# High and low weight halves made by GpSimd's DMAs instead of ScalarE and VectorE, in a decoder block on one core

## The chip, the cores and the metric

The kernel runs on one core of a Trainium2 chip. The metric is device time in microseconds (us) of one execution; a figure for a kernel is the median over its runs. The profile comes from one execution, taken by the hardware profiler. Engines are named as in the profile: PE (TensorE matmul), PEld (its weight load), DVE (VectorE), ACT (ScalarE), POOL (GpSimd), SP (SyncE, which here only issues DMAs).

## The reference

One decoder layer on 512 tokens of width 1024, all in float32. Cut to what matters:

```python
h  = rms_norm(x, norm_mix_g)
glu_in, q, k, v, g, gate_logits = split(h @ w_in)
a  = conv31(glu_in[:, :1024] * sigmoid(glu_in[:, 1024:]))     # causal, depthwise
y_a = silu(layer_norm(a)) @ w_conv_proj + conv_proj_b
r  = retention(rotary(q) / 16, rotary(k), v)                   # 4 heads, dk 256, dv 512
y_b = (silu(g) * head_norm(r) * ret_norm_g) @ w_ret_proj
x  = x + (sigmoid(gA) * y_a + sigmoid(gB) * y_b) @ w_out
u  = conv3(rms_norm(x, norm_ffn_g) @ w_up)                     # causal, depthwise
x  = x + (silu(u[:, :3072]) * u[:, 3072:]) @ w_down
return rms_norm(x, norm_final_g)
```

All matrices together are 24.1 million weights, 96.5 MB in float32.

## The kernel before, in words

**Layout.** Activations lie transposed: 128 features on the partitions, 512 tokens in a row. A product is made in *units*: one PSUM bank of 128 output features by 512 tokens, summed over the K blocks of 128 input features (`unit`, L142).

**Split numbers.** PE multiplies in the type float32r, which keeps fewer digits than float32. So each weight and each activation is kept as two float32r tiles, the value rounded (high half, `whi`, `xg` and others) and the rest (low half, `wlo`), and each product is three matmuls: high by high, high by the activation's low half, low by high (L146 to L148).

**The weight stream.** The host lays the weights out in the order of use, in 184 pieces ("halves" in the code) of 128 x 1024 floats, 512 KB each, eight 128 x 128 blocks. One piece feeds 24 matmuls, for most products just one unit. `load_half` (L92) lets SP load a piece into a tile `wraw` (3 buffers). `split_half` (L99) lets ACT round it into `whi` (L105, 3 buffers) and DVE subtract that from `wraw` into `wlo` (L106, 3 buffers). `blocks` (L118) hands out the blocks and, when piece h comes into use, makes sure that pieces up to h + 2 have been asked for (`LOOK = 2`). A buffer comes free when PE has done the last matmul that reads it. Pieces 0 and 1 are asked for at the start, between the loads of x.

**Order.** A scheduler orders the instructions of each engine by priority and its own idea of when they are ready; each engine then works its list strictly in order, and an instruction that waits holds up all that stand behind it on its engine. The pieces have a raised priority (`WPRIO`), the taps of the 31-tap convolution a much lowered one (L337, 30 DVE instructions for each of 8 channel blocks), so that they fill what DVE has left.

**Stages.** For each of four heads: two gated channel blocks (4 units) and their convolution taps, q and k with rotation, the projection of the head before, values, scores, the gate, the retention products. Then the gates, the projections, `w_out`, 28 units of `w_up`, half of `w_down`, 20 more units of `w_up`, the rest of `w_down`, the last norm. Each norm needs a sum over partitions: PE adds with a matrix of ones (L190), DVE scales, POOL takes the power -0.5 (L206), DVE splits, and a unit later PE spreads the result over the partitions (L221). POOL otherwise only clears the few columns ahead of each convolution's input (`ap`, 3 buffers, L327 and L551); that waits until the taps that read the buffer before are done.

Of the kernel before, what the change touches and what calls it, by code (L numbers as in the profile page):

```python
# [9 lines left out]
F32 = mybir.dt.float32  # L10
F32R = mybir.dt.float32r
AF = mybir.ActivationFunctionType
ALU = mybir.AluOpType

P = 128
# [10 lines left out]
FK = 3  # L26
EPS = 1e-6
HS = 8 * P
LOOK = 2
WARM = 9  # L30
WPRIO = 100

# columns of the packed per-feature parameters
_PC = {}
_n = 0
for _name, _w in (
# [11 lines left out]
def hybrid_block(  # L48
# [10 lines left out]
    nc = tc.nc  # L59
    sb = ctx.enter_context(tc.tile_pool(name="sb", bufs=1))  # L60
# [3 lines left out]
    def nm(s):  # L64
        uid[0] += 1
        return f"{s}_{uid[0]}"

    def t512(tag, bufs, dt=F32):
        return sb.tile([P, S], dt, tag=tag, bufs=bufs, name=nm(tag))
# [4 lines left out]
    def bank():  # L74
        return psp.tile([P, S], F32, tag="ps", name=nm("ps"))

    def f32(ap):
        return ap.bitcast(F32)
# [4 lines left out]
        c = _PC[name] + i  # L83
        return par[:, c:c + 1]

# [1 line left out]
    halves = {}  # L87
    emitted = [0]

    raws = {}  # L90

    def load_half(h):  # L92
        raw = sb.tile([P, HS], F32, tag="wraw", bufs=3, name=nm("wraw"))
        cut = (0, 2 * P, HS) if h == 0 else (0, HS)
        raws[h] = raw, [slice(u, v) for u, v in zip(cut, cut[1:])]
        for sl in raws[h][1]:
            nc.sync.dma_start(out=raw[:, sl], in_=wst[h][:, sl])

    def split_half(h):  # L99
        raw, sls = raws.pop(h)  # L100
        hi = sb.tile([P, HS], F32R, tag="whi", bufs=3, name=nm("whi"))
        lo = sb.tile([P, HS], F32R, tag="wlo", bufs=3, name=nm("wlo"))
        with tc.high_priority(offset=WPRIO if h > 1 else 0):
            for sl in sls:
                nc.scalar.copy(out=hi[:, sl], in_=raw[:, sl])  # L105
                nc.vector.tensor_tensor(out=lo[:, sl], in0=raw[:, sl], in1=f32(hi[:, sl]),  # L106
                                        op=ALU.subtract)
        halves[h] = (hi, lo)

    def upto(h):  # L110
        while emitted[0] <= min(h, NBLK - 1):
            load_half(emitted[0])
            split_half(emitted[0])
            emitted[0] += 1

    pos = [0]
# [1 line left out]
    def blocks(n):  # L118
        b = pos[0]
        pos[0] += n  # L120
        h, c = divmod(b, 8)
        upto(h + LOOK)
        hi, lo = halves[h]
        sl = slice(c * P, (c + n) * P)
        return hi[:, sl], lo[:, sl]
# [3 lines left out]
    def later(n, fn):  # L129
        pending.append([n, fn])  # L130
# [42 lines left out]
    def split_scaled(src, g, tag, bufs):  # L173
        h = t512(tag, bufs, F32R)
        l = t512(tag, bufs, F32R)
        nc.scalar.activation(out=h, in_=src, func=AF.Copy, scale=g)
        nc.vector.scalar_tensor_tensor(
            out=l, in0=src, scalar=g, in1=f32(h), op0=ALU.mult, op1=ALU.subtract)
        return h, l
# [1 line left out]
    def add_into(acc, v):  # L181
        nc.vector.tensor_tensor(out=acc, in0=acc, in1=v, op=ALU.add)  # L182

# [1 line left out]
    def tok_sums(ps, parts, chunks=range(NCH), at=0):  # L185
        """The sums of parts over their partitions: token c * 128 + p's at [p, at + c]."""
        last = len(parts) - 1
        for c in chunks:
            for i, (ss, o) in enumerate(parts):
                nc.tensor.matmul(ps[:, at + c:at + c + 1], lhsT=ss[:, c * P - o:(c + 1) * P - o],  # L190
                                 rhs=ones[:, 0:1], start=i == 0, stop=i == last)

    def tok(dt=F32):
        if dt == F32R:
            return sb.tile([P, NCH], F32R, tag="tokr", bufs=4, name=nm("tokr"))
        return sb.tile([P, NCH], F32, tag="tok", bufs=8, name=nm("tok"))

    def scaled(ps, n, eps, sl=slice(0, NCH)):
        o = tok()
        nc.vector.tensor_scalar(out=o[:, sl], in0=ps[:, sl], scalar1=1.0 / n, scalar2=eps,  # L200
                                op0=ALU.mult, op1=ALU.add)
        return o

    def rsqrt(v, sl=slice(0, NCH)):
        r = tok()
        nc.gpsimd.tensor_tensor(out=r[:, sl], in0=v[:, sl], in1=neghalf[:, sl], op=ALU.pow)  # L206
        return r

    def spread_ps(ps, r, chunks=range(NCH)):
        """r's value of each token, on every partition."""  # L210
        sl = slice(chunks[0], chunks[-1] + 1)
        rh = tok(F32R)
        rl = tok(F32R)
        nc.vector.tensor_copy(out=rh[:, sl], in_=r[:, sl])
        nc.vector.tensor_tensor(out=rl[:, sl], in0=r[:, sl], in1=f32(rh[:, sl]), op=ALU.subtract)

        def run():
            for c in chunks:
                dst = ps[:, c * P:(c + 1) * P]
                for i, x in enumerate((rh, rl)):  # L220
                    nc.tensor.matmul(dst, lhsT=x[:, c:c + 1].broadcast_to([P, P]), rhs=identr,  # L221
                                     start=i == 0, stop=i == 1)
            return ps

        return run
# [4 lines left out]
        return b  # L230

    def stat(ss, n, eps, use, wait=(2, 1)):
        """use(spread, per token) of rsqrt(sum / n + eps), or of the mean where eps is None."""
        def second():
            ps = bank()
            tok_sums(ps, [(ss, 0)])
            v = scaled(ps, n, eps or 0.0)
            r = v if eps is None else rsqrt(v)
            run = spread_ps(ps, r)
            later(wait[1], lambda: use(run, r))  # L240

        later(wait[0], second)

# [1 line left out]
    ones = sb.tile([P, P], F32, tag="ones", name="ones")  # L245
    nc.gpsimd.memset(ones, 1.0)
    neghalf = sb.tile([P, NCH], F32, tag="neghalf", name="neghalf")
# [8 lines left out]
    for i in range(KT):  # L256
        t = t512("x", 8)
        nc.sync.dma_start(out=t, in_=xT[i * P:(i + 1) * P, :])
        xs.append(t)
        if i == 0:  # L260
            nc.sync.dma_start(out=g0, in_=params[:, _PC["norm_mix_g"]:_PC["norm_mix_g"] + KT])
            load_half(0)
        if i == 3:
            load_half(1)
    ident = sb.tile([P, P], F32, tag="ident", name="ident")
    nc.sync.dma_start(out=ident, in_=ident_in)
    nc.sync.dma_start(out=par, in_=params)
# [2 lines left out]
    xg = []  # L270
    for i in range(KT):
        xg.append(split_scaled(xs[i], g0[:, i:i + 1], "xg", 16))
        if i in (0, 3):
            split_half(emitted[0])
            emitted[0] += 1

# [31 lines left out]
        nc.vector.tensor_tensor(out=t, in0=ps, in1=rB[0], op=ALU.mult)  # L308
        return t

# [1 line left out]
    PAD = CONV_K - 1  # L312
    accs = [None] * KT
    csum = [None]
# [9 lines left out]
    def glu(ta, sg):  # L324
        nc.scalar.activation(out=sg, in_=sg, func=AF.Sigmoid)
        a = sb.tile([P, S + PAD], F32, tag="ap", bufs=3, name=nm("ap"))
        nc.gpsimd.memset(a[:, 0:PAD], 0.0)  # L327
        nc.vector.tensor_tensor(out=a[:, PAD:], in0=ta, in1=sg, op=ALU.mult)
        return a
# [39 lines left out]

        stat(csum[0], D, None, centre, (3, 2))  # L370

# [1 line left out]
    def rope():  # L373
        p1 = unit(bank(), xg)
        p2 = unit(bank(), xg)
        res = []
        for u, v, op in ((p1, p2, ALU.subtract), (p2, p1, ALU.add)):
            m1 = tmp()
            m2 = tmp()
            nc.vector.tensor_tensor(out=m1, in0=u, in1=cosr, op=ALU.mult)  # L380
            nc.vector.tensor_tensor(out=m2, in0=v, in1=sinr, op=ALU.mult)
            nc.vector.tensor_tensor(out=m1, in0=m1, in1=m2, op=op)
            res.append(split(m1, "A", 16))
        return res
# [97 lines left out]
            else:  # L482
                add_into(yb[m], ps)

# [1 line left out]
    stat(ss.acc, D, EPS, norm_mix)  # L486
    rg = None
    for h in range(H):
        ps = [glu_units() for _ in range(2)] if h else glu_first()
        for i in range(2):  # L490
            a = glu(*ps[i])
# [50 lines left out]
        x1g.append(split_scaled(x_, pcol("norm_ffn_g", m), "A", 16))  # L542
        ss.add(x_)

# [1 line left out]
    def norm_ffn(run, _):  # L546
        rB[0] = spread(run, "rB", 1)

# [68 lines left out]
    def finish(half):  # L617
# [7 lines left out]
        def early(sqs):  # L625
            for q in sqs:
                add_into(ss.acc[:, tk], q[:, :HT])
            tok_sums(ps, [(ss.acc, 0)], chunks)
            part.append(scaled(ps, D, EPS, sl))

        def first(sqs):
            tok_sums(ps, [(sqs[-1], half * HT)], chunks, NCH)
            v = tok()
            nc.vector.scalar_tensor_tensor(
                out=v[:, sl], in0=ps[:, NCH + sl.start:NCH + sl.stop], scalar=1.0 / D,
                in1=part[0][:, sl], op0=ALU.mult, op1=ALU.add)
            run.append(spread_ps(ps, rsqrt(v, sl), chunks))
# [22 lines left out]

# [1 line left out]
def _units(w):  # L662
    """Blocks of 128 output features, each with its K rows: (n, 128, K/128 * 128)."""
    k, n = w.shape
    return w.reshape(k // P, P, n // P, P).transpose(2, 1, 0, 3).reshape(n // P, P, k)

# [94 lines left out]
```

## Time and profile before

| | |
|---|---|
| runs | 1097.77 and 1098.85 us, median 1098.31 us |
| span of the profiled execution, first to last instruction | 1096.1 us |
| median of the runs less this span | 2.2 us |
| PE busy | 1084.7 us, 99% of the span |
| DVE busy | 760.4 us, 69% |
| ACT busy | 419.9 us, 38% |
| POOL busy | 20.5 us, 2% |
| DMA queue of SP | 104.69 MB, 29.0% of 16 DMA engines' time |

How to read it: the span is what the trace covers; the 2.2 us beside it are what the timed runs have on top of it. A busy PE is not PE at its peak, since matmuls overlap in the pipeline. Waiting, issuing a DMA and branching do not count as busy.

### The profile page before, as it was taken

To read this page: it belongs to the slowest core of one execution; us is meant where nothing else is said; L and a number is where in the kernel's file an instruction comes from. 1 tells how busy PE (TensorE), PEld (TensorE's weight loads), DVE (VectorE), ACT (ScalarE), POOL (GpSimd) and SP (SyncE) were. 2 spreads that over 40 slices of the span, in tenths; PEclk is the share of its full clock that TensorE was granted. 3 is DMA by queue.
4 is the path that set the end of the run, shared out by engine and by line. 5 is a ranking of instruction groups with operands and counts; after the bars stand their busy time and mean duration, and the time that the engine had idled before them with its cause. 6 is when DMAs were issued, how large, how long until landed. Compare 5 with 4: busy or idle time off the path is not lost.

```text
span 1096.1 us, 12567 instructions
## 1 busy us (share of the span) xinstructions
PE 1084.7 (99%) x4946; PEld 895.9 (82%) x4946; DVE 760.4 (69%) x1070; ACT 419.9 (38%) x555; POOL 20.5 (2%) x72
## 2 busy tenths in 40 slices
PE   8999999999999999999999999999999999999997
PEld 7888888888888888888888888888888888888886
DVE  6999699739995699938664555577676226767433
ACT  6343332534233331535552334444443113444331
POOL 1000000000000000000000000000000000000000
PEclk9999999999999999999999999999999999999998
DMA  7232132222222232222232432222232222233212
GB/s 271 97 97 87 62 111 91 93 68 86 97 96 87 71 102 96 78 77 77 84 109 94 138 122 100 84 97 97 96 97 92 94 92 90 94 97 96 96 58 77
DMA packets 32475, 105.48 MB, mean 96 GB/s; under 512 B 3616, under 2 KB 5920, under 8 KB 32416
## 3 DMA queue, kind: packets, MB, share of 16 engines
q1 hardware_dynamic: 32416, 104.69, 29.0%
q8 instruction: 38, 0.62, 0.2%
q14 instruction: 21, 0.17, 0.1%
HBM read 102.58 MB, written 2.10 MB: 95 GB/s over the span
## 4 chain that ended last, share of the span: by engine, by line
PE 97%; issue 1%; DVE 1%; DMA 0%; SPq 0%; ACT 0%; POOLq 0%; POOL 0%; DVEq 0%
PE ps L146 28%; PE ps L148 27%; PE ps L147 27%; PE ps L393 3%; PE ps L395 3%; PE ps L394 3%; PE ps L451 1%; PE ps L452 1%; PE ps L450 1%; PE ps L221 1%; PE ps L190 1%; PE ps L429 0%; PE ps L427 0%; PE ps L425 0%; DMA wraw<-in_wst_dram 0%
## 5 line engine op out<-in xcount | busy, mean ns | idle before, releaser
L105 ACT CAST whi<-wraw 128x1024 fp32r<-128x1024 f32 (+1 forms) x185 | 193.6, 1047 | 427.8 <-PE ps L147 296.3
L106 DVE TENSOR_TENSOR wlo<-wraw,whi 128x1024 fp32r<-128x1024 f32 (+1 forms) x185 | 225.0, 1216 | 71.0 <-ACT whi L105 70.2
L146 PE MATMUL ps<-xg,whi 128*128 128x512 f32 x672 | 263.4, 392 | 0.0
L148 PE MATMUL ps<-xg,wlo 128*128 128x512 f32 x672 | 261.8, 390 | 0.0
L147 PE MATMUL ps<-xg,whi 128*128 128x512 f32 x672 | 261.5, 389 | 0.0
L146 PE MATMUL ps<-A,whi 128*128 128x512 f32 x448 | 177.1, 395 | 0.0
L148 PE MATMUL ps<-A,wlo 128*128 128x512 f32 x448 | 177.0, 395 | 0.0
L337 DVE SCALAR_TENSOR_TENSOR C<-ap,par,C 128x512 f32<-128x512 f32 x240 | 166.3, 745 | 3.1 <-ACT C L334 2.7
L147 PE MATMUL ps<-A,whi 128*128 128x512 f32 x384 | 151.7, 395 | 0.0
L148 PEld LDWEIGHTS ps<-xg,wlo 128*128 128x128 f32 x672 | 126.1, 188 | 27.0
L147 PEld LDWEIGHTS ps<-xg,whi 128*128 128x128 f32 x672 | 126.2, 188 | 25.9
L146 PEld LDWEIGHTS ps<-xg,whi 128*128 128x128 f32 x672 | 126.2, 188 | 25.7
L148 PEld LDWEIGHTS ps<-A,wlo 128*128 128x128 f32 x448 | 84.0, 187 | 20.5
L146 PEld LDWEIGHTS ps<-A,whi 128*128 128x128 f32 x448 | 84.0, 187 | 20.4
L147 PEld LDWEIGHTS ps<-A,whi 128*128 128x128 f32 x384 | 72.0, 187 | 17.6
L308 DVE TENSOR_TENSOR t<-ps,rB 128x512 f32<-128x512 f32 x48 | 32.5, 687 | 72.3 <-PE ps L148 72.3
L558 DVE SCALAR_TENSOR_TENSOR t<-ap,par,t 128x512 f32<-128x512 f32 x96 | 71.5, 749 | 1.6
L182 DVE TENSOR_TENSOR x<-x,ps 128x512 f32<-128x512 f32 (+1 forms) x50 | 33.0, 664 | 54.8 <-PE ps L148 51.0
L552 DVE TENSOR_TENSOR ap<-ps,rB 128x512 f32<-128x512 f32 x48 | 33.0, 692 | 47.3 <-PE ps L148 47.3
L146 PE MATMUL ps<-R,whi 128*128 128x512 f32 x160 | 63.3, 396 | 0.0
L148 PE MATMUL ps<-R,wlo 128*128 128x512 f32 x160 | 63.2, 395 | 0.0
L147 PE MATMUL ps<-R,whi 128*128 128x512 f32 x160 | 63.2, 395 | 0.0
(135 smaller groups left out, 1181.8 us busy)
## 6 DMA issues: line engine op xcount, KB each, us to landing
wraw<-in_wst_dram SPq DMA_DIRECT2D x183, 512.0 KB, 3.3
x<-in_xT_dram SPq DMA_DIRECT2D x16, 256.0 KB, 3.4
out_dram<-t SPq DMA_DIRECT2D x8, 256.0 KB, 2.2
dec<-in_decay_dram SPq DMA_DIRECT2D x4, 256.0 KB, 2.6
t<-in_cs_dram SPq DMA_DIRECT2D x2, 256.0 KB, 4.7
wraw<-in_wst_dram SPq DMA_DIRECT2D x1, 384.0 KB, 4.0
par<-in_params_dram SPq DMA_DIRECT2D x1, 264.0 KB, 6.2
wraw<-in_wst_dram SPq DMA_DIRECT2D x1, 128.0 KB, 3.5
```

The source lines that it names most:

```text
L105: nc.scalar.copy(out=hi[:, sl], in_=raw[:, sl])
L106: nc.vector.tensor_tensor(out=lo[:, sl], in0=raw[:, sl], in1=f32(hi[:, sl]), op=ALU.subtract)
L146: nc.tensor.matmul(ps, lhsT=wh, rhs=xh, start=kt == 0, stop=False)
L147: nc.tensor.matmul(ps, lhsT=wh, rhs=xl, start=False, stop=False)
L148: nc.tensor.matmul(ps, lhsT=wl, rhs=xh, start=False, stop=kt == last)
L182: nc.vector.tensor_tensor(out=acc, in0=acc, in1=v, op=ALU.add)
L337: nc.vector.scalar_tensor_tensor(out=acc, in0=a[:, k:k + S], scalar=wcol(k), in1=acc, op0=ALU.mult, op1=ALU.add)
L393: nc.tensor.matmul(banks[c], lhsT=xh[:, sl], rhs=wh, start=kt == 0, stop=False)
L394: nc.tensor.matmul(banks[c], lhsT=xl[:, sl], rhs=wh, start=False, stop=False)
L395: nc.tensor.matmul(banks[c], lhsT=xh[:, sl], rhs=wl, start=False, stop=kt == KT - 1)
L552: nc.vector.tensor_tensor(out=u[:, FK - 1:], in0=ps, in1=rB[0], op=ALU.mult)
L558: nc.vector.scalar_tensor_tensor(out=c, in0=u[:, k:k + S], scalar=wcol(k), in1=c, op0=ALU.mult, op1=ALU.add)
```

## The change

Only piece 0 still comes through `wraw`, ACT and DVE (`ON_ENGINES = 1`; `wraw` keeps one buffer). Pieces 1 to 183 go through `split_by_dma`: a DMA that GpSimd issues reads the piece from memory and writes it as float32r into `whi`; ACT writes the negated `whi` into `wlo`; a second DMA of GpSimd reads the same piece from memory again and adds it onto `wlo`. `whi` and `wlo` have four buffers each instead of three, and `LOOK` is 3. ACT's rounding (1024 columns) has thus become a negation (1024 columns), and DVE's subtraction is gone for 183 pieces; SP issues 183 fewer DMAs and POOL 366 more, and the weights are read from memory twice.

```diff
-LOOK = 2
+LOOK = 3
+ON_ENGINES = 1
...
-        raw = sb.tile([P, HS], F32, tag="wraw", bufs=3, name=nm("wraw"))
+        raw = sb.tile([P, HS], F32, tag="wraw", bufs=ON_ENGINES, name=nm("wraw"))
...
+    def w_tiles():
+        return (sb.tile([P, HS], F32R, tag="whi", bufs=LOOK + 1, name=nm("whi")),
+                sb.tile([P, HS], F32R, tag="wlo", bufs=LOOK + 1, name=nm("wlo")))
+
     def split_half(h):
         raw, sls = raws.pop(h)
-        hi = sb.tile([P, HS], F32R, tag="whi", bufs=3, name=nm("whi"))
-        lo = sb.tile([P, HS], F32R, tag="wlo", bufs=3, name=nm("wlo"))
-        with tc.high_priority(offset=WPRIO if h > 1 else 0):
...
+    def split_by_dma(h):
+
+        hi, lo = w_tiles()
+        with tc.high_priority(offset=WPRIO):
+            nc.gpsimd.dma_start(out=hi, in_=wst[h])
+            nc.scalar.activation(out=lo, in_=f32(hi), func=AF.Copy, scale=-1.0)
+            nc.gpsimd.dma_start(out=lo, in_=wst[h], accum_op=ALU.add)
         halves[h] = (hi, lo)
 
     def upto(h):
         while emitted[0] <= min(h, NBLK - 1):
-            load_half(emitted[0])
-            split_half(emitted[0])
+            split_by_dma(emitted[0])
             emitted[0] += 1
...
-        if i == 3:
-            load_half(1)
...
-        if i in (0, 3):
+        if i == 0:
             split_half(emitted[0])
```

**Where the instructions stand.** POOL's list at the start, before the change: after the first clearings it has only the identity's cast and the first power.

```order
L327 MEMSET ap_1166 128x30
L269 CAST identr<-ident 128x128
L206 ISA
L206 TENSOR_TENSOR tok_243<-tok_241,neghalf 128x4
L327 MEMSET ap_1203 128x30
```

POOL's list at the same place with the change; `whi_170`, `whi_175` and `whi_180` are pieces 1 to 3, `whi_209` is piece 4 and `whi_252` piece 5.

```order
L336 MEMSET ap_1150 128x30
L117 DMA whi_170<-in_wst_dram 128x1024
L117 DMA whi_175<-in_wst_dram 128x1024
L117 DMA whi_180<-in_wst_dram 128x1024
L119 DMA wlo_171<-in_wst_dram 128x1024
L119 DMA wlo_176<-in_wst_dram 128x1024
L119 DMA wlo_181<-in_wst_dram 128x1024
L117 DMA whi_209<-in_wst_dram 128x1024
L278 CAST identr<-ident 128x128
L117 DMA whi_252<-in_wst_dram 128x1024
L119 DMA wlo_210<-in_wst_dram 128x1024
L217 TENSOR_TENSOR tok_245<-tok_243,neghalf 128x4
```

The three casting DMAs of pieces 1 to 3 are issued before anything that waits; the adding ones follow behind ACT's negations; the identity's cast and the first power now stand behind DMAs.

ACT's list at the start with the change, from the rounding of piece 0 (`whi_108`) on; `xg` are the high halves of the scaled x, and `t_144` the first of the squares for the norm.

```order
L108 CAST whi_108<-wraw_82 128x768
L187 ACTIVATE xg_114<-x_85,g_78 128x512
L292 ACTIVATE t_144<-x_85 128x512
L187 ACTIVATE xg_118<-x_87,g_78 128x512
L118 ACTIVATE wlo_171<-whi_170 128x1024
L187 ACTIVATE xg_122<-x_89,g_78 128x512
L118 ACTIVATE wlo_176<-whi_175 128x1024
L187 ACTIVATE xg_126<-x_91,g_78 128x512
L118 ACTIVATE wlo_181<-whi_180 128x1024
L187 ACTIVATE xg_130<-x_93,g_78 128x512
L292 ACTIVATE t_147<-x_87 128x512
```

Before, one instruction of this size (the rounding of piece 1) stood among the eight `xg`, and the squares stood between them; now three negations stand there, and five of the squares come after the last `xg`.

POOL's list among the 28 units of `w_up`, before the change: clearings only.

```order
L551 MEMSET ap_5730 128x2
L551 MEMSET ap_5737 128x2
L551 MEMSET ap_5812 128x2
L551 MEMSET ap_5819 128x2
```

The same place with the change, for one pair of units (pieces `whi_5715` and `whi_5745`) and the start of the next.

```order
L117 DMA whi_5715<-in_wst_dram 128x1024
L560 MEMSET ap_5854 128x2
L117 DMA whi_5745<-in_wst_dram 128x1024
L119 DMA wlo_5716<-in_wst_dram 128x1024
L560 MEMSET ap_5861 128x2
L119 DMA wlo_5746<-in_wst_dram 128x1024
L117 DMA whi_5795<-in_wst_dram 128x1024
```

The first piece's adding DMA stands behind the second piece's casting one, and both stand behind clearings that wait for DVE's taps.

## Rows read from the trace of the kernel before

**Rows 1.** The page: span, busy time by engine, chain that ended last.
```profile
span 1096.1 us, 12567 instructions
PE 1084.7 (99%) x4946; PEld 895.9 (82%) x4946; DVE 760.4 (69%) x1070; ACT 419.9 (38%) x555; POOL 20.5 (2%) x72
...
PE 97%; issue 1%; DVE 1%; DMA 0%; SPq 0%; ACT 0%; POOLq 0%; POOL 0%; DVEq 0%
```

**Rows 2.** PE's waits, longest: line, released by, us in total, times, longest.
```profile
PE ps L221 <- DVE tokr L214: 1.2, 1, 1.2
PE ps L253 <- POOL neghalf L248: 1.0, 1, 1.0
...
PE ps L160 <- DVE xg L177: 0.9, 2, 0.6
```

**Rows 3.** Windows: busy time by engine, granted PE clock, DMA share, GB/s.
```profile
0.00:20.00 20.00, 16.77 (x76) 13.47 (x77) 14.14 (x20) 15.80 (x24) 1.95 (x10) 1.00 0.77 279
...
900.00:1000.00 100.00, 100.00 (x430) 80.41 (x429) 66.36 (x82) 40.08 (x50) 1.62 (x16) 1.00 0.29 95
```

**Rows 4.** Groups by form: busy us, mean ns of one, idle before and its releasers.
```profile
L106 DVE TENSOR_TENSOR wlo<-wraw,whi 128x1024 fp32r<-128x1024 f32 x183 | 223.6, 1222 | 69.8 <-ACT whi L105 69.0 <-issue 0.3
...
L105 ACT CAST whi<-wraw 128x1024 fp32r<-128x1024 f32 x183 | 192.4, 1052 | 426.7 <-PE ps L147 296.3 <-issue 75.1 <-PE ps L394 45.3
```

**Rows 5.** DMA: SP's queue, and two issues (count, KB, us to landing).
```profile
q1 hardware_dynamic: 32416, 104.69, 29.0%
...
wraw<-in_wst_dram SPq DMA_DIRECT2D x183, 512.0 KB, 3.3
...
par<-in_params_dram SPq DMA_DIRECT2D x1, 264.0 KB, 6.2
```

**Rows 6.** Timeline of ACT among the units of `w_up`: start, duration.
```profile
760.93 1.05 ACT L105 CAST whi<-wraw 128x1024 fp32r<-128x1024 f32 x1 [1.17 <-PE ps L147]
...
766.53 1.05 ACT L105 CAST whi<-wraw 128x1024 fp32r<-128x1024 f32 x1 [0.46 <-PE ps L147]
...
772.13 1.05 ACT L105 CAST whi<-wraw 128x1024 fp32r<-128x1024 f32 x1 [1.17 <-PE ps L147]
```

**Rows 7.** Timeline at the start: SP's issue and ACT.
```profile
4.02 0.43 SPq L97 DMA_DIRECT2D wraw<-in_wst_dram  x1
...
6.17 0.83 ACT L105 CAST whi<-wraw 128x768 fp32r<-128x768 f32 x1 [0.60 <-DMA wraw<-in_wst_dram]
...
10.32 1.03 ACT L105 CAST whi<-wraw 128x1024 fp32r<-128x1024 f32 x1
...
15.20 0.71 ACT L176 ACTIVATE xg<-x,g 128x512 fp32r<-128x512 f32 x1
```

**Rows 8.** Timeline at the start: PE, and DVE's subtraction of piece 1.
```profile
8.71 0.50 PE L160 MATMUL ps<-xg,whi 128*128 128x512 f32 x1 [0.30 <-DVE xg L177]
...
11.70 1.22 DVE L106 TENSOR_TENSOR wlo<-wraw,whi 128x1024 fp32r<-128x1024 f32 x1
...
13.64 0.50 PE L160 MATMUL ps<-xg,whi 128*128 128x512 f32 x1 [0.56 <-DVE xg L177]
...
15.15 0.39 PE L160 MATMUL ps<-xg,whi 128*128 128x512 f32 x1
...
18.83 0.95 PE L190 MATMUL ps<-ones,ss 128*128 128x1 f32 x8
```

**Rows 9.** Timeline of POOL.
```profile
106.80 0.12 POOL L327 MEMSET ap<- 128x30 f32 x1 [2.33 <-DVE C L337]
120.56 1.01 POOL L206 TENSOR_TENSOR tok<-tok,neghalf 128x4 f32<-128x4 f32 x1 [13.64 <-DVE tok L200]
...
206.29 0.12 POOL L327 MEMSET ap<- 128x30 f32 x1 [9.15 <-DVE C L337]
243.51 1.96 POOL L206 TENSOR_TENSOR tok<-tok,neghalf 128x4 f32<-128x4 f32 x1 [37.09 <-DVE tok L200]
```

**Rows 10.** Timeline of PE: a norm's sum and spread, and head 1's first gate unit.
```profile
119.34 0.94 PE L190 MATMUL ps<-ones,ss 128*128 128x1 f32 x8
...
125.73 1.01 PE L221 MATMUL ps<-identr,tokr 128*128 128x128 f32 x8
...
201.81 0.46 PE L146 MATMUL ps<-xg,whi 128*128 128x512 f32 x1
```

**Rows 11.** Timeline of ACT at the end: the last piece's rounding.
```profile
1067.20 1.05 ACT L105 CAST whi<-wraw 128x1024 fp32r<-128x1024 f32 x1 [4.43 <-PE ps L147]
```

More of the change, by code (lines that the diff above doesn't have):

```diff
@@ L97, in load_half @@
             nc.sync.dma_start(out=raw[:, sl], in_=wst[h][:, sl])
+    def w_tiles():
+        return (sb.tile([P, HS], F32R, tag="whi", bufs=LOOK + 1, name=nm("whi")),
+                sb.tile([P, HS], F32R, tag="wlo", bufs=LOOK + 1, name=nm("wlo")))
     def split_half(h):
         raw, sls = raws.pop(h)
-        hi = sb.tile([P, HS], F32R, tag="whi", bufs=3, name=nm("whi"))
-        lo = sb.tile([P, HS], F32R, tag="wlo", bufs=3, name=nm("wlo"))
-        with tc.high_priority(offset=WPRIO if h > 1 else 0):
[L104 to L107, printed above, removed]
+        hi, lo = w_tiles()
+        for sl in sls:
+            nc.scalar.copy(out=hi[:, sl], in_=raw[:, sl])
+            nc.vector.tensor_tensor(out=lo[:, sl], in0=raw[:, sl], in1=f32(hi[:, sl]),
+                                    op=ALU.subtract)
+        halves[h] = (hi, lo)
+    def split_by_dma(h):
+        hi, lo = w_tiles()
+        with tc.high_priority(offset=WPRIO):
+            nc.gpsimd.dma_start(out=hi, in_=wst[h])
+            nc.scalar.activation(out=lo, in_=f32(hi), func=AF.Copy, scale=-1.0)
+            nc.gpsimd.dma_start(out=lo, in_=wst[h], accum_op=ALU.add)
         halves[h] = (hi, lo)
```

## The prediction

> **What bounds the kernel now.** I read the page first. PE is busy for 99% of the span, and PE makes 97% of the chain that ended last [rows 1]. Then PE's waits: the longest is 1.2 us, and the next are 1.0 and 0.9 us [rows 2]; nothing on the list repeats from piece to piece. The windows show the same in the middle as over the whole: PE is busy for all of a stretch of 100 us, with DVE at 66, ACT at 40, POOL at 2 and the DMA engines at 29 of 100; the granted clock is 1.00 there and in the first 20 us, which is the upper of PE's two levels (2.4 GHz) [rows 3]. Last the pace: in `w_up` ACT rounds a piece every 5.60 us, and each time it has waited for matmuls to give up a buffer [rows 6]. So the weight stream runs at the pace of the matmuls, and a piece may take 5.6 us of any other resource before that resource sets the time. Work taken from DVE or ACT is taken from beside the path. The one place where weights and activations are on the path is the start: matmuls wait 0.30 and 0.56 us for DVE there [rows 8].
>
> **What goes.** 183 subtractions of 1.222 us, 223.6 us of DVE [rows 4]. DVE falls from 760 to about 537 us, 49% of the span. All of it lies beside matmuls, but for piece 1's at 11.70, ahead of which PE has nothing better to wait for: DVE's high and low halves of x are late by 0.56 us at 13.64 [rows 8]. I put the gain at 0 to 1.2 us. SP loses 183 issues of 0.43 us [rows 7], which nobody waits for.
>
> **What is exchanged.** ACT's rounding, 183 times 1.052 us [rows 4], becomes a negation of the same shape. The nearest row of ACT with a scale is the `xg` of half the size, 0.71 us [rows 7], which bounds it from above by twice that, 1.4 us; I take 1.05 to 1.1. ACT is at 38% and the path isn't on it: 0.
>
> **What is added, first price: the DMA engines.** No row shows a DMA that casts or adds, or one that GpSimd issues. The price of a plain piece does show: SP's queue took 29.0% of the span for 104.69 MB [rows 5], so a piece of 0.524 MB takes 0.290 x 1096.1 x 0.524 / 104.69 = 1.59 us of all 16 engines. The crowded first 20 us, 0.77 busy at 279 GB/s [rows 3], give 0.77 x 0.524 MB / 279 GB/s = 1.45 us. The casting DMA moves the same bytes in and out: I take 1.59. The adding one moves at least that; call it k times 1.59. It has to fetch the piece and the old value and to write the sum. k = 1 is the lower end, k = 3 (fetch, fetch and write, each as dear as a whole copy) the upper; I take k = 2: if a copy takes as long as its one read stream, two streams take twice that. Then a piece takes 1.59 + 3.18 = 4.8 of the 5.6 us that it has, 85%: still hidden, with little left over. At k = 1 it is 57%. The engines set the pace from (1 + k) x 1.59 > 5.6, so k above 2.5, and at k = 3 a piece takes 6.37 us. The first matmul came at 8.71 us [rows 8] and the last piece's rounding 28.9 us before the span's end [rows 1, 11], so some 35 us lie outside the stream: 183 x 6.37 + 35 = 1201 us. Between, k = 2.7 makes 183 x 5.9 + 35 = 1112.
>
> On this the Trainium skill has a rule ("Collectives: The Full Stack", The bandwidth ceiling: the fold count and why AG ≠ RS ≠ AR): an add in the DMA engine needs two source reads, and its reduce-scatter was measured at 32.35 GB/s against 62.28 for the gather, 1.93 times dearer. No run here shows that; by it the pair of DMAs would take 1.59 x 2.93 = 4.7 us a piece (an estimate from that page), and the sum stays as it is.
>
> **Second price: latency and POOL's list.** SP's 512 KB land 3.3 us after issue, and 6.2 us where they queue behind others [rows 5]. An issue by GpSimd lies, I think, between SP's 0.43 us [rows 7] and POOL's longest instruction, 1.96 us [rows 9]; I take 1. In `w_up` a pair of pieces has 11.2 us. Let T be the moment when a's buffer comes free; with four buffers a is needed three pieces on, at T + 16.8. Cast a is issued by T + 1 and lands by T + 4.3, the negation is done by T + 5.4. The add must stand behind cast b, whose buffer comes free at T + 5.6: cast b issued by 6.6, add a by 7.6, landed by 10.9, or by 14.2 with twice the time under way. That leaves 2.6 to 5.9 us. Cast b lands by 9.9, its negation ends at 11.0, add b is issued by 12.0 and lands by 15.3 to 18.6, with 22.4 as the due time: 3.8 to 7.1 us. POOL's loop is about 8 us of 11.2. So this is 0 as long as a casting DMA lands within some 8 us.
>
> Other work on POOL now stands behind these waits. A norm's power: the sum on PE at 119.34, the power on POOL at 120.56 for 1.01 us [rows 9], the spread on PE at 125.73 [rows 10]. With DVE's split between, 3 us are free, and one issue ahead of the power takes 1 to 2: 0. If the DMA ahead of it still waits for its buffer, that could grow to a piece's 5.6 us at a norm, which the forecast's range takes in once. Clearings of `ap` wait for DVE's taps, 2.33 us at 106.80 and 9.15 us at 206.29 [rows 9]; the adds behind them wait too. Head 1's first gate unit began at 201.81 [rows 10], and at three heads an add of a piece that is used about then stands behind that clearing. But the taps fill what DVE has left, and DVE loses the subtractions of some 18 pieces over those 100 us, 22 us: they end near 184, and the add goes out in time. 0.
>
> **Third price: the start.** Here nothing is hidden. Before, one further piece was issued at 4.02 [rows 7], behind half of x. Now POOL issues three at about 1 us. They share the engines with x: 2 x 0.524 MB more, at 279 GB/s [rows 3], is 3.8 us until x is there. On ACT two more 1024-column instructions, 2.1 us, stand ahead of the last `xg`, which began at 15.20 [rows 7]. Piece 1 is in use at 15.15, after the 24 matmuls of piece 0 that began at 8.71 [rows 8]; its low half is there only after the cast has landed (behind x, 6 us or more from 1, as `par` [rows 5]), the negation among the `xg` near 10.3 [rows 7], an issue of 1 us and 3.3 to 6.2 us more: 15 to 18.5. The squares, too, come later to the sums at 18.83 [rows 8]. These delays run side by side, not one after another. I take 3.5 us, near the 3.8; the ends are 3.8 + 3.5 = 7.3, if the add queues behind a late x, and -1.2, if DVE's relief is all that shows. At the end nothing changes: the last rounding is at 1067.20 [rows 11], and its successor's DMAs have the stretch before it.
>
> **The sum.** The profiled execution's span of 1096.1 us and 2.2 us around it make 1098.3, the median of the runs. 1098.3 + 0 (DVE, ACT, SP) + 0 (DMA engines at k = 2) + 0 (POOL) + 3.5 (start) = 1101.8, say 1102. Its own range is 1097 to 1109, the bounds of the start and part of that 5.6 us.
>
> **Rivals.** (1) *The adding DMA becomes the bound*, the slower side: k above 2.5. For it: three moves instead of two, at a queue that nobody has seen, and a margin of only 15% at k = 2. Against it: the engines stand at 29%, and a copy already carries a read and a write within its 1.59 us. PE would then wait for a DMA of `wlo` in every piece, and the time be 1201 at k = 3; it passes 2% at k = 2.75 or so. (2) *POOL's waits hold up the weights*: if the taps end no earlier than before, the add behind the clearing of 206.29 goes out at 207.3 and lands at 210.6, 8.8 us behind 201.81 [rows 9, 10]; at three heads 26 us, so 1102 + 26 = 1128. For it: the waits of 9.15 us; against it: DVE's 22 us. (3) *A cheaper start*: the casts land early, since they are issued before x is asked for, DVE is free for x, and the time is 1098.3 - 1.2 = 1097. Against it: the bytes of x have to come all the same. (4) *A real gain* has no place in the profile: PE is idle for 1096.1 - 1084.7 = 11.4 us in all [rows 1], 8.71 of them ahead of the first matmul [rows 8], and its pace is its own.
>
> **How the numbers follow.** The forecast (1097 to 1109) 0.64, the cheaper start 0.05, the DMA bound 0.24 (0.21 of it above 2%), POOL's waits 0.05, a gain of over 2% 0.02. The likeliest gives 1102. The range goes from 1097 to 1190: the forecast, about half of the cheaper start, POOL's waits and a part of the DMA bound, some 0.8. 1190 is k = 2.95. A measurement of this kernel tells about 2% from no change, that is 1076 to 1120. Faster 0.02; within 2% 0.64 + 0.05 + 0.03 = 0.72; slower 0.21 + 0.05 = 0.26.
>
> **What would show it.** Right: PE at 98% or more, no wait for a DMA after the first 30 us, ACT's negations 5.6 us apart, GpSimd's queue at 70 to 90% of the engines' time or less, adds that land under 7 us, DVE near 537 us, taps of the first head that end near 184, the sums of x's norm at 21 to 24 instead of 18.83. Wrong: a wait of PE on a DMA of `wlo` in each piece with the engines near 100% (rival 1, k from the queue's share), or with POOL late and the engines idle (rival 2, or a dear issue: above 2.8 us for each of four, POOL's pair no longer fits into 11.2 us).

## The result, and the profile after

The changed kernel took 1245.85 us (median; 1244.04 to 1247.65) against 1098.31: 1.134 times the time before, 95% interval 1.132 to 1.136. The forecast was 1102 us with a range up to 1190, so it was wrong in size and beyond its range, and the mechanism that I gave most of the slower side to, the adding DMA as a bound of the DMA engines, isn't the one that struck.

The page of the changed kernel: span, busy time, GpSimd's DMA queue, the chain that ended last, and the two kinds of DMA (count, KB, us to landing). They answer to [rows 1] and [rows 5].

```profile
span 1245.9 us, 12692 instructions
PE 1134.3 (91%) x4946; PEld 912.3 (73%) x4946; DVE 548.9 (44%) x887; ACT 410.2 (33%) x555; POOL 275.6 (22%) x438
...
q0 software_dynamic: 52704, 191.91, 67.0%
...
DMA 17%; issue 12%; PE 9%; ACT 4%; POOL 3%; DVE 2%; POOLq 0%; DVEq 0%; ACTq 0%
...
whi<-in_wst_dram POOLq DMA_DIRECT2D x183, 512.0 KB, 6.5
wlo<-in_wst_dram POOLq DMA_DIRECT2D x183, 512.0 KB, 5.5
```

PE is idle for 111.6 us where it was idle for 11.4, and PE's share of the chain is 9% where it was 97% (the page follows this chain back to 660 us only, so its shares add up to 47%). But the DMA engines are busy for only 67% of the span with the weights. Nothing is full. Next the waits (line, released by, us in total, times, longest), which answer to [rows 2]:

```profile
POOL wlo L119 <- ACT wlo L118: 792.2, 173, 10.4
ACT wlo L118 <- DMA whi<-in_wst_dram: 399.6, 94, 9.0
...
PE ps L159 <- DMA wlo<-in_wst_dram: 70.0, 51, 3.3
...
POOL whi L117 <- PE ps L159: 16.4, 10, 5.6
```

PE waits for adding DMAs, POOL waits for 792 of 1246 us with an adding DMA at its head whose negation isn't there, and ACT waits with that negation for a casting DMA to land. The last line tells the most: a casting DMA hardly ever waits for a free buffer, ten times in 183 by this line and twice by others of the view; 16.7 of these 24.2 us lie in the first 50 us. After that, when a casting DMA reaches the head of POOL's list, its buffer has as a rule long been free. The look-ahead of three pieces isn't used.

The windows (columns as in [rows 3]):

```profile
0.00:20.00 20.00, 13.20 (x48) 9.94 (x49) 8.61 (x13) 13.48 (x21) 6.21 (x17) 1.00 0.95 304
20.00:120.00 100.00, 99.09 (x459) 82.93 (x458) 68.15 (x115) 32.41 (x47) 21.92 (x32) 0.98 0.71 163
120.00:220.00 100.00, 93.84 (x404) 76.15 (x403) 65.56 (x104) 33.45 (x47) 24.06 (x35) 0.97 0.69 161
...
620.00:720.00 100.00, 88.83 (x370) 69.60 (x369) 29.34 (x44) 28.41 (x37) 21.15 (x31) 0.98 0.75 181
```

After the start, PE keeps up for a hundred microseconds and then falls behind. I read that as a lead of three pieces being eaten up by a stream that is a little too slow, not as a single stall.

POOL's timeline in that later stretch (start, duration, what it waited for):

```profile
650.71 0.85 POOL L119 DMA_DIRECT2D wlo<-in_wst_dram  x1 [6.87 <-ACT wlo L118]
651.25 1.42 POOL L117 DMA_DIRECT2D whi<-in_wst_dram  x2
658.76 0.88 POOL L119 DMA_DIRECT2D wlo<-in_wst_dram  x1 [6.08 <-ACT wlo L118]
660.32 0.86 POOL L119 DMA_DIRECT2D wlo<-in_wst_dram  x1 [0.69 <-ACT wlo L118]
660.87 0.87 POOL L117 DMA_DIRECT2D whi<-in_wst_dram  x1
670.40 0.85 POOL L119 DMA_DIRECT2D wlo<-in_wst_dram  x1 [8.67 <-ACT wlo L118]
670.95 1.42 POOL L117 DMA_DIRECT2D whi<-in_wst_dram  x2
```

This is how the loss comes about. POOL issues two casting DMAs (651.25), stands still until the first has landed and ACT has negated it (658.76), issues two adding ones, then one casting one (660.87), and stands still again (670.40). While it stands no casting DMA goes out. Three pieces take 670.95 - 651.25 = 19.7 us, where three units of PE's work take 3 x 5.6 = 16.8 [rows 6].

### The profile page after: what moved, and what is told of

Its sections match the earlier page's. It is cut to its first block, busy times and chain, and to the rows that moved or that the text cites. A ratio compares the mean times of both kernels' runs of the same rounds, so it can differ in the third digit from the quotient of the medians.

```text
span 1245.9 us, 12692 instructions
## 1 busy us (share of the span) xinstructions
PE 1134.3 (91%) x4946; PEld 912.3 (73%) x4946; DVE 548.9 (44%) x887; ACT 410.2 (33%) x555; POOL 275.6 (22%) x438
## 5 line engine op out<-in xcount | busy, mean ns | idle before, releaser
L118 ACT ACTIVATE wlo<-whi 128x1024 fp32r<-128x1024 f32 x183 | 193.4, 1057 | 651.3 <-DMA whi<-in_wst_dram 399.6
L119 POOL DMA_DIRECT2D wlo<-in_wst_dram x183 | 158.0, 863 | 859.1 <-ACT wlo L118 792.2
L159 PE MATMUL ps<-xg,wlo 128*128 128x512 f32 x672 | 269.1, 400 | 36.6 <-DMA wlo<-in_wst_dram 36.6
L157 PE MATMUL ps<-xg,whi 128*128 128x512 f32 x672 | 268.4, 399 | 3.4 <-ACT t L411 1.8
L158 PE MATMUL ps<-xg,whi 128*128 128x512 f32 x672 | 266.7, 397 | 0.7 <-DVE xg L181 0.7
L159 PE MATMUL ps<-A,wlo 128*128 128x512 f32 x448 | 181.7, 406 | 22.3 <-DMA wlo<-in_wst_dram 22.2
L157 PE MATMUL ps<-A,whi 128*128 128x512 f32 x448 | 179.5, 401 | 3.2 <-ACT A L187 3.2
L158 PE MATMUL ps<-A,whi 128*128 128x512 f32 x384 | 153.7, 400 | 0.0
L157 PEld LDWEIGHTS ps<-xg,whi 128*128 128x128 f32 x672 | 129.1, 192 | 31.2 <-ACT t L411 2.7
L158 PEld LDWEIGHTS ps<-xg,whi 128*128 128x128 f32 x672 | 128.8, 192 | 28.8 <-DVE xg L181 1.6
L117 POOL DMA_DIRECT2D whi<-in_wst_dram x183 | 137.8, 806 | 34.7 <-PE ps L159 16.4
L193 DVE TENSOR_TENSOR ss<-ss,t 128x512 f32<-128x512 f32 (+1 forms) x40 | 27.2, 680 | 95.1 <-ACT t L292 93.0
L157 PE MATMUL ps<-R,whi 128*128 128x512 f32 x160 | 64.8, 405 | 0.0
L158 PE MATMUL ps<-R,whi 128*128 128x512 f32 x160 | 64.8, 405 | 0.0
```

The costliest lines, as they stand in the source:

```text
L117: nc.gpsimd.dma_start(out=hi, in_=wst[h])
L118: nc.scalar.activation(out=lo, in_=f32(hi), func=AF.Copy, scale=-1.0)
L119: nc.gpsimd.dma_start(out=lo, in_=wst[h], accum_op=ALU.add)
L157: nc.tensor.matmul(ps, lhsT=wh, rhs=xh, start=kt == 0, stop=False)
L158: nc.tensor.matmul(ps, lhsT=wh, rhs=xl, start=False, stop=False)
L159: nc.tensor.matmul(ps, lhsT=wl, rhs=xh, start=False, stop=kt == last)
```

## The experiments

**Theory A**: the round trip on POOL sets the pace. An adding DMA waits at POOL's head for a landing and a negation, and the next casting DMAs stand behind it. **Theory B**: the adding DMAs are too dear for the DMA engines, or hold the stream up as such. **Rival C**: ACT is late with the negations for other work. **Rival D**: adding alone, in any order. A *trip* below runs from the first casting DMA that POOL issues after an adding one to the next such; a trip of one or of two has that many casting DMAs in it.

**e1: the second DMA doesn't add.**

```diff
-            nc.gpsimd.dma_start(out=lo, in_=wst[h], accum_op=ALU.add)
+            nc.gpsimd.dma_start(out=lo, in_=wst[h])
```

> The second DMA of each piece writes the rounded piece over the negation without adding, so the low halves are wrong and no old value is fetched; order, waits and the negation stay. Theory A (the round trip on POOL: the next casting DMAs stand behind adding ones that wait for a landing and a negation): the waits are the same and only the fetch of the old value goes, so 1200 to 1250 us. Theory B (the adding DMA is too dear for the DMA engines): without the add the time falls below 1150 us.

1104.05 us, 1.0066 times before (1.0042 to 1.0089). That was theory B's number, and A's expectation missed. The page, GpSimd's queue and the DMAs' landings:

```profile
q0 software_dynamic: 52704, 191.91, 56.4%
...
whi<-in_wst_dram POOLq DMA_DIRECT2D x183, 512.0 KB, 4.6
wlo<-in_wst_dram POOLq DMA_DIRECT2D x183, 512.0 KB, 4.0
```

A casting DMA costs 0.564 x 1102.3 / 366 = 1.70 us of all 16 engines. And without adds it lands after 4.6 us (median) instead of 6.5. So the experiment changed two things that I had taken for one: the engines' work and the length of the trip. The other experiments had to part them.

**e2: no negation, so no wait on POOL between a piece's two DMAs.** Four fixed low tiles, the same 183 adds.

```diff
             nc.gpsimd.dma_start(out=hi, in_=wst[h])
-            nc.scalar.activation(out=lo, in_=f32(hi), func=AF.Copy, scale=-1.0)
             nc.gpsimd.dma_start(out=lo, in_=wst[h], accum_op=ALU.add)
```

> The negation is left out: the adding DMAs add onto what four fixed low tiles held, so the low halves are wrong; all DMAs, adding ones too, stay, and POOL no longer waits for ACT between a piece's two DMAs. Theory A: the casting DMAs go out as soon as buffers come free, 1100 to 1125 us. Theory B: the same bytes and the same adds, 1220 to 1250 us, with the DMA share as before, near 67%.

1113.49 us, 1.0139 (1.0119 to 1.0160). The page and the longest wait:

```profile
q0 software_dynamic: 52704, 191.91, 84.0%
...
POOL whi L126 <- PE ps L167: 621.6, 162, 11.7
```

All adds are there, the DMA engines are busier than in the changed kernel (84 against 67%), and the stream keeps up: now the casting DMAs wait for PE's buffers, as they should. Theory B in its first form, that the engines can't carry the adds, is out. The pair of DMAs takes 0.840 x 1111.8 / 183 = 5.10 us of the engines, the adding one by itself 5.10 - 1.70 = 3.40. (PE is busy for 1097.3 us in e2, 12.6 more than before, in a stream without waits; that was not followed up.)

**e3: nothing left out, another order on POOL.** Each adding DMA is queued behind the next piece's casting one.

```diff
         with tc.high_priority(offset=WPRIO):
-            nc.gpsimd.dma_start(out=hi, in_=wst[h])
-            nc.scalar.activation(out=lo, in_=f32(hi), func=AF.Copy, scale=-1.0)
-            nc.gpsimd.dma_start(out=lo, in_=wst[h], accum_op=ALU.add)
+            cast = nc.gpsimd.dma_start(out=hi, in_=wst[h])
+        waiting.append((h, hi, lo))
+        if len(waiting) > 1:
+            add_low(getattr(cast, "ins", cast))
...
```

`add_low` emits the negation of piece h - 1 and its adding DMA, the latter behind `cast`.

> Nothing is left out; on POOL each piece's adding DMA now stands behind the next piece's casting one, so that a casting DMA is under way while POOL waits for the negation of the piece before. Theory A: the round trip of a piece overlaps the next one's, 1100 to 1130 us, PE's waits for DMAs of wlo nearly gone after the start. Theory B: no change, 1220 to 1250 us.

1110.81 us, 1.0117 (1.0100 to 1.0134): 135 of the 148 us are back, by the order alone, which puts each negation one piece later, too. The waits, and the windows of the middle:

```profile
POOL whi L129 <- PE ps L175: 514.8, 152, 11.7
...
POOL wlo L123 <- ACT wlo L118: 81.7, 96, 10.3
```

```profile
120.00:1000.00 880.00, 880.00 (x3949) 723.57 (x3948) 441.05 (x693) 333.14 (x436) 226.78 (x356) 1.00 0.87 183
```

POOL's wait for negations falls from 792 to 82 us, and PE is busy for every microsecond from 120 to 1000 with the DMA engines at 87%.

**e4: the adding DMA alone**, with SP's load and ACT's rounding, three buffers and two pieces ahead as before the change.

```diff
-LOOK = 3
+LOOK = 2
...
-            nc.gpsimd.dma_start(out=hi, in_=wst[h])
...
+            nc.sync.dma_start(out=raw, in_=wst[h])
+            nc.scalar.copy(out=hi, in_=raw)
```

> One part alone: the high half is rounded by ACT from a piece that SP loads (three buffers of each, two pieces ahead, as before the change), ACT also writes the negation, and a DMA of GpSimd adds the piece onto it. The piece is still read twice and added 183 times; POOL has no casting DMAs. Theory A: SP's loads run ahead by themselves, so a piece costs one landing behind the negation, 1098 to 1120 us. Theory B: the adds set the pace, above 1200 us.

1114.14 us, 1.0145 (1.0125 to 1.0166). 183 adds, and no slow stream: SP's list runs ahead by itself. The adding DMAs wait at POOL's head for their negations even longer than in the changed kernel, but no load of a piece stands behind them, and the stream loses nothing by it. PE's idle time has moved to the start, where ACT has more to do ahead of the high halves of x (line, released by, us, times, longest):

```profile
POOL wlo L121 <- ACT wlo L120: 838.9, 178, 13.8
...
PE ps L172 <- ACT xg L189: 11.1, 2, 6.6
```

**e5: casting and adding DMAs strictly in turn**, one casting DMA to a trip, where the changed kernel, counted over POOL's whole timeline, has 56 trips with one casting DMA, 62 with two and one with three.

```diff
-            nc.gpsimd.dma_start(out=hi, in_=wst[h])
...
+                with tc.issue_after(last_add[0]):
+                    nc.gpsimd.dma_start(out=hi, in_=wst[h])
...
```

> Nothing is left out; on POOL every casting DMA now stands behind the adding one of the piece before, so casting and adding DMAs strictly alternate, where the changed kernel has mostly two casting ones or one between adding ones. Theory A (round trip on POOL): a round trip for each piece, by the changed kernel's trace 6.2 to 7.5 us of landing, 1.4 us of negation and up to 1 us of issue, so 8.6 to 9.5 us: 183 times that and 35 us make 1600 to 1770 us. Theory B2 (the adds as such hold the stream up, by engine time): the same DMAs, so within 2% of 1246 us.

1534.85 us, 1.398 (1.395 to 1.401). The same DMAs, a quarter slower again; POOL's timeline:

```profile
670.47 0.87 POOL L125 DMA_DIRECT2D wlo<-in_wst_dram  x1 [6.66 <-ACT wlo L124]
671.02 0.88 POOL L123 DMA_DIRECT2D whi<-in_wst_dram  x1
678.43 0.86 POOL L125 DMA_DIRECT2D wlo<-in_wst_dram  x1 [6.53 <-ACT wlo L124]
678.98 0.87 POOL L123 DMA_DIRECT2D whi<-in_wst_dram  x1
```

A trip is 678.98 - 671.02 = 8.0 us here, and (1535 - 35) / 183 = 8.2 on average. I had expected 8.6 to 9.5, and so 1600 to 1770 us: the time went the way of theory A, but by less than its range. Those numbers were from trips of the changed kernel, in which a casting DMA often stands behind two adds.

**e6: the negations on DVE.**

```diff
-            nc.scalar.activation(out=lo, in_=f32(hi), func=AF.Copy, scale=-1.0)
+            nc.vector.tensor_scalar(out=lo, in0=f32(hi), scalar1=-1.0, scalar2=None, op0=ALU.mult)
```

> Nothing is left out; the changed kernel with its negations on DVE instead of ACT. Theory A: POOL still issues no casting DMA while it waits for a landing and a negation, so 1180 to 1260 us. Rival C (the negations come late because they stand behind ACT's other work, and the landing is no matter): 1100 to 1140 us.

1351.97 us, 1.231 (1.229 to 1.234): outside both, and the reason lies in the list. Counted over POOL's timeline, the scheduler now put one casting DMA into 104 trips, two into 38 and three into one: 143 trips instead of 119. With 8.2 us for a trip of one, e6 gives (1352 - 35 - 104 x 8.2) / 39 = 11.9 us for a trip of two or three. The changed kernel by these two numbers: 56 x 8.2 + 63 x 11.9 + 35 = 1244 us; it took 1246. Its own trace has both kinds: a trip of one behind a trip of one takes 8.4 us (mean of 19), a trip of two behind a trip of two 11.9 (25). Where the two alternate, they take 9.4 and 10.5 (36 each), together 19.9 us for three pieces. Rival C is out as the main cause: e3 leaves the negations on ACT among its other work and brings the time back, and in e6, without ACT's other work ahead of them, the time rose (though DVE's work now stands there).

**e7: the casting DMA alone**, SP loading the piece for DVE's subtraction, three buffers and two pieces ahead, as before the change.

```diff
-            nc.scalar.activation(out=lo, in_=f32(hi), func=AF.Copy, scale=-1.0)
-            nc.gpsimd.dma_start(out=lo, in_=wst[h], accum_op=ALU.add)
...
+            nc.sync.dma_start(out=raw, in_=wst[h])
+            nc.vector.tensor_tensor(out=lo, in0=raw, in1=f32(hi), op=ALU.subtract)
```

> One part alone: the high half comes from a casting DMA of GpSimd, SP loads the piece as well, and DVE subtracts as before the change; three buffers, two pieces ahead. Theory A: POOL waits for buffers only, 1098 to 1110 us with the start's cost. Theory B in the form that GpSimd's DMAs as such are slow: above 1150 us.

1107.34 us, 1.0086 (1.0057 to 1.0115). GpSimd's DMAs aren't slow as such: they land after 3.9 us here, and POOL waits mainly for buffers that PE gives up (598.6 us).

**e9: e5's order with e1's DMAs**, the one that parts theory A from rival D. Against e5:

```diff
-            add = nc.gpsimd.dma_start(out=lo, in_=wst[h], accum_op=ALU.add)
+            add = nc.gpsimd.dma_start(out=lo, in_=wst[h])
```

> The order of e5 (casting and second DMAs strictly alternate on POOL), and the second DMA writes the rounded piece without adding, as in e1, so the low halves are wrong. Theory A with a shorter trip as the reason for e1: in e1's trace a trip with one casting DMA takes 6.65 us from one casting issue to the next, against 8.2 us in e5, and a piece has 5.9 us on average; so 183 x 6.65 + 35 = 1250 us, between 1190 and 1260. Rival D (it is the adding as such, its fetch of the old value, that holds up the stream, and without it the order is no matter): 1100 to 1115 us as e1.

1250.00 us, 1.138 (1.136 to 1.140), where A's sum was 1250 (1252 by its own terms) and D's 1100 to 1115. No DMA adds anything, the engines are at 47%, and the kernel is as slow as the changed one (that the two times nearly agree is chance, as the lists differ). POOL's timeline:

```profile
667.18 0.53 POOL L125 DMA_DIRECT2D wlo<-in_wst_dram  x1 [5.54 <-ACT wlo L124]
667.70 0.54 POOL L123 DMA_DIRECT2D whi<-in_wst_dram  x1
673.63 0.53 POOL L125 DMA_DIRECT2D wlo<-in_wst_dram  x1 [5.39 <-ACT wlo L124]
674.15 0.54 POOL L123 DMA_DIRECT2D whi<-in_wst_dram  x1
```

A trip of 6.45 us (6.7 on average over the timeline) against PE's 5.6. So e1 was cured because its trips got short enough, with two casting DMAs in about half of them, and not because nothing was added. e1's own waits agree: its casting DMAs wait for buffers, as those of the changed kernel hardly do.

```profile
POOL whi L117 <- PE ps L159: 188.7, 64, 7.7
```

The loss takes both: this order on POOL, and trips that the adds make long. Without the adds (e1) or in the other order (e3) most of it is gone.

**e8 and e10: the rest of e3.** e8 is e3 with pieces 0 and 1 through SP, ACT and DVE, and POOL's first casting DMA behind the identity's cast; e10 takes piece 2 that way too (`ON_ENGINES` is 3 there).

```diff
-ON_ENGINES = 1
+ON_ENGINES = 2
...
+            with tc.issue_after(getattr(ident_cast[0], "ins", ident_cast[0])):
+                cast = nc.gpsimd.dma_start(out=hi, in_=wst[h])
...
```

> Nothing is left out; casting DMAs one piece ahead on POOL as in e3, and the start as before the change: pieces 0 and 1 come through SP, ACT and DVE, and POOL's first casting DMA stands behind the identity's cast, so behind the loads of x. Theory A with the start as the rest: 1097 to 1101 us, no change against before. If e3's last 1% lies elsewhere in the stream: 1106 to 1112 us as e3.

> Nothing is left out; e8 with piece 2, too, through SP, ACT and DVE, since PE waited 2.5 us for its adding DMA in e8. Theory A with the start as the rest: 1097 to 1101 us, within 0.3% of before; nothing in the stream is left to gain, as PE sets the pace.

1103.20 us (1.0046, 1.0030 to 1.0063), 2 us above what was expected of e8, and 1100.12 us (1.0017, 1.0008 to 1.0026), as expected. PE's timeline at the start in e3, then in e10:

```profile
19.65 1.00 PE L188 MATMUL ps<-xg,wlo 128*128 128x512 f32 x2 [2.68 <-DMA wlo<-in_wst_dram]
26.75 1.05 PE L217 MATMUL ps<-ones,ss 128*128 128x1 f32 x8 [0.65 <-DVE ss L209]
```

```profile
8.87 0.50 PE L192 MATMUL ps<-xg,whi 128*128 128x512 f32 x1 [0.30 <-DVE xg L209]
19.70 1.05 PE L222 MATMUL ps<-ones,ss 128*128 128x1 f32 x8 [1.07 <-DVE ss L214]
```

The sums of x's norm come at 26.75 in e3 and at 19.70 in e10, against 18.83 before [rows 8]. All that e10 changes against e3 lies at the start, so 10.7 of e3's 12.8 us are the start by the medians (7.7 between the two profiled executions, as e3's runs spread from 1107.0 to 1111.4). None of the versions beats the kernel before: with the order mended, PE sets the pace again.

## Why the prediction was wrong, step by step

**What bounds the kernel, what goes, what is exchanged** held. DVE fell to 549 us (537 forecast) and nothing was won by it; the negation takes 1.057 us (1.05 to 1.1). In e10 PE is busy for 1085.1 us, as in [rows 1]. One row was misread: 8.71 us is not the first matmul of piece 0 but a later one that waited. The first stood here:

```profile
5.62 0.73 PE L159 MATMUL ps<-xg,whi 128*128 128x512 f32 x2 [0.97 <-ACT whi L105]
```

PE was idle for 2.7 us before 8.71, not for 8.71. Little hangs on it: 5.62 and 28.9 make 34.5 us outside the stream, the 35 that the sums use, and rival 4 stands without it.

**The DMA engines' price** held. I took 1.59 us for the casting DMA and k = 2, 4.8 us a pair; e1 and e2 give 1.70 and 3.40 us, 5.1 a pair, so k = 2.1. The price was lower where the engines were less full: the pair took 4.5 in e5 (54%), and less the 1.59 of a casting DMA in the same order (e9) that leaves 2.9 for the add, 1.85 times as much. At 87% of the engines (85 forecast) e3's stream has no wait. The rule of the Trainium skill ("Collectives: The Full Stack", The bandwidth ceiling: the fold count and why AG ≠ RS ≠ AR), that an add reads two sources, gave 1.93 times a copy (a reduce-scatter against a gather). These runs, with 1.85 to 2.0 times a casting copy, agree. Rival 1 didn't happen, and couldn't at this k. (By the prediction's formula 1190 us is k = 2.97, not 2.95.)

**The step that failed** is in the second price, "latency and POOL's list": "Cast a is issued by T + 1", with T the release of its buffer, and from it "POOL's loop is about 8 us of 11.2. So this is 0 as long as a casting DMA lands within some 8 us." It landed after 6.5 (median), and yet most of the 148 us went here: another order of the list gave 135 back. Three things were wrong in it. The casting DMA isn't issued when its buffer is free but when POOL has got past the former adds, and these wait for a landing; the loop closes on itself, and the buffers' lead doesn't enter. A landing was priced at 3.3 us, with the engines to itself (the 6.2 that stood beside it is the row of `par`, 264 KB and not 512); right behind an adding DMA it is 6.1 to 6.5. The same order without adds has 4.6 (e9 against e5), so the adds lengthen it; that it is their engine time ahead of it in the queue that does so fits the 3 us each, but wasn't tested apart. And I read one place of the list, with pairs, and took it for all of them. Here is that place, `w_up`, in the changed kernel:

```profile
832.82 0.88 POOL L117 DMA_DIRECT2D whi<-in_wst_dram  x1
834.46 0.10 POOL L560 MEMSET ap<- 128x2 f32 x1 [0.77 <-DVE t L567]
835.00 0.55 POOL L117 DMA_DIRECT2D whi<-in_wst_dram  x1 [0.44 <-issue]
840.44 0.88 POOL L119 DMA_DIRECT2D wlo<-in_wst_dram  x1 [4.89 <-ACT wlo L118]
842.64 0.10 POOL L560 MEMSET ap<- 128x2 f32 x1 [1.32 <-DVE t L567]
844.41 0.86 POOL L119 DMA_DIRECT2D wlo<-in_wst_dram  x1 [1.67 <-ACT wlo L118]
844.96 0.87 POOL L117 DMA_DIRECT2D whi<-in_wst_dram  x1
```

The loop that was put at 8 us takes 844.96 - 832.82 = 12.1, for 11.2 of PE's. Pairs alone would have made about 183 x 6.1 + 35 = 1151 us (an estimate from this loop); the rest are the 56 trips of one piece, which take 8.4 to 9.4 us for 5.6. The text gave a point from which the wait decides, 8 us of landing; worked out as a loop it would have been about 5 (an estimate): a trip of one and a trip of two, 19.9 us for three pieces, are 3.1 us over PE's 16.8, or 1.5 us for each of the two landings of 6.5.

**Rival 2** named POOL's order, and the sign given for it, PE waiting for `wlo` with POOL late and the engines not full, did come (its other reading, a dear issue, is out: POOL issued a DMA every 0.55 us, where 1 us was taken). But its price was the clearings and DVE's taps as what holds up the adds. In the trace it is the negations: 792 us of waiting. The clearings of `w_up` wait for DVE, too, 44.6 us in all, and stand inside the loop above; what they add to it wasn't tested apart, but e3 keeps them and PE doesn't wait there. The taps do end earlier, about as forecast: with the start put back (e10) the clearing of 206.29 [rows 9] comes at 188.34, 18 us sooner, where 22 were forecast.

**The third price, the start**, was too low: 3.5 us forecast, with 7.3 as the upper end. In the changed kernel the sums of x's norm came at 25.91 us, 7.1 late, and putting the start back was worth 10.7 us of timed runs between e3 and e10. The late x and the late add don't run side by side, as I had it; they add up in part. The first casts had landed by about 11 us (8.5 us from issue at most), but ACT's first negation began only at 12.23, behind `xg` instructions one of which waited for x until 10.47; the add went out at 13.58, and PE waited 2.63 us for it at 19.65.

## What to carry to other kernels

Where one in-order queue issues both a transfer and a second transfer that depends on the first, the look-ahead counts only up to the first waiting instruction in that queue: work out the loop of issue, landing, dependent step and issue, divide by the first transfers in one turn of it, and compare with the time that the consumer takes for a piece. Engines far from full and a producer that hardly ever waits for a free buffer are the sign of such a loop; the wait at the queue's head by itself is not, as e4 has more of it at no cost. The cure here was the order in the queue (more buffers weren't tried). Count the turns over the whole list, since a scheduler may group the transfers differently from stage to stage.

## What the runs showed of the hardware

For 512 KB an adding DMA of GpSimd took 2.9 to 3.4 us of the 16 engines (3.2 alone in e4), a casting one 1.6 to 1.7 (e9, e7, e1), SP's plain one 1.59 [rows 5]. On POOL the row of an adding DMA lasts 0.86 us, but the next issue starts 0.55 us after it; the row of a casting one lasts 0.55 us, or 0.87 right behind an adding one. Landings go with what was issued just before: the median of the casting DMAs was 3.9 us among plain loads (e7), 4.6 among casting ones (e1, e9), 6.1 to 6.5 right behind adding ones (the changed kernel, e5, e6), and 4.9 to 5.4 where the last add went out some microseconds before (e2, e3, e8, e10).

PE's granted clock fell after some of its waits. In the changed kernel it was 0.78 in the window of 765 to 770 us, a mixture of its two levels (2.4 and 1.2 GHz), and PE's timeline shows both, in the duration of one matmul:

```profile
765.00:770.00 5.00, 3.20 (x10) 2.52 (x11) 0.60 (x2) 0.00 (x0) 0.00 (x0) 0.78 1.06 247
```

```profile
763.24 0.39 PE L158 MATMUL ps<-xg,whi 128*128 128x512 f32 x1
766.80 0.50 PE L159 MATMUL ps<-xg,wlo 128*128 128x512 f32 x1 [3.18 <-DMA wlo<-in_wst_dram]
...
767.85 0.63 PE L157 MATMUL ps<-xg,whi 128*128 128x512 f32 x1
...
771.25 0.39 PE L159 MATMUL ps<-xg,wlo 128*128 128x512 f32 x1
```

A microsecond after a wait of 3.18 us the matmuls run at 0.63 us instead of 0.39, until 771. Part of the 49.6 us by which PE is busier than before is that; whether it lengthened the kernel or lies within time that PE would have waited anyway wasn't tested apart. That the casting DMAs hardly wait for buffers that PE gives up speaks for the second.
